# A second SwiGLU FFN on one core: where the differences and splits of the hidden tiles are queued

## The chip, the cores and the metric

The kernel runs on one core of one Trainium2 chip. A core has five engines, each with an instruction queue of its own that it works through in order: TensorE (PE in the profile; its weight loads are PEld), VectorE (DVE), ScalarE (ACT), GpSimd (POOL) and SyncE (SP). [...] The metric is the time of one execution on the device in microseconds; several executions are timed and the median is given. One more execution is recorded by the hardware profiler, and every view of the trace comes from that one.

## The reference, cut to what matters

One layer of a hybrid model in float32: 128 context tokens and 512 latent tokens (640 in all), 1024 channels; a SwiGLU FFN, a mixer, a second SwiGLU FFN, a last norm. The change is in the second FFN, whose hidden width is 2816.

```python
def swiglu(h, w1, w2):
    a, b = jnp.split(h @ w1, 2, axis=-1)
    return (jax.nn.silu(a) * b) @ w2

    h = modulate(rmsnorm(x, norm_g[2]), sh2, sc2)
    x = x + 0.5 * g2[:, None, :] * swiglu(h, ffn2_w1, ffn2_w2)
```

## The kernel before

**Products.** Channels lie on the 128 partitions, tokens on the free axis; the 640 tokens are two halves of 320. Each float32 operand is split into a high part (a cast to the type that TensorE reads, `A.copy` on ScalarE, line 75) and a low part (the difference, `V.tensor_sub` on VectorE, line 79). `three` (lines 245 to 247) multiplies high by high, high by low and low by high into the same accumulator `ps`.

**A pair.** Two weight columns (`mi` 0 and 1) times two token halves (`h` 0 and 1) is a 2 by 2 block product. `pair_steps` does it with seven products in place of eight, by sums and differences of blocks. The seven steps, numbered 0 to 6, are A11, S1, S2, A12, S3, S4, A22; each is 12 matmuls of 320 columns. The weight sums (`ws`, line 218) are made on VectorE, and each weight operand is split ahead of its use: the call of `op()` at a step queues the cast and the difference of the operand four steps on. The operands on the token side are tiles named 11, T1, T2, 21, T3, 22 and T4, in the order of the steps.

Between the products stand copies on ScalarE and additions on VectorE. After step 0 ScalarE copies the accumulator a to b (L273), which S2 then adds to; after step 1 it copies one to an SBUF tile (L279); after step 2 it copies b to c (L283), which S3 adds to. L294 (or L291 and L292) and L297 are additions on VectorE after S3 and S4. The results go through `ev`. Two of them are put off (the list `late`) and run by `flush()` behind the next pair's L273. Four accumulators rotate, so that a product may have to wait until an old one has been read; the one that S1 writes is free when L297 of the pair before has read it.

**Groups of eight.** In the second FFN the hidden width runs in groups of 8, 8 and 6 tiles. `eights` builds the first two: eight hidden tiles j, each a pair with the two halves of its w1 columns (tiles 0 and 1 of group 0 are done elsewhere, in the head, so `n_head` is 2), and then four pairs with w2 (m = 0, 2, 4, 6). The results of the hidden tiles are the token operands of the w2 pairs, so their differences are needed as well, and each operand is split. That work is put in the list `lazy` as closures: `left` and `diff1` for tiles 0 to 3 (one cast and one VectorE operation; one cast and two), `diff2`, `diff3` and `diff4` for tiles 4 to 7 (one cast and two VectorE operations each). They are added to `lazy` when a pair's results are complete, which is at `flush()` in step 0 of the next pair. T3 and T4 go to tiles lent from other operands (`put_lent`).

**When `lazy` runs.** In `pair_el`, a pair that is not `calm` calls `relax(7 - i)` behind step i from 1 on: it runs closures until fewer than 7 − i are left, so two closures run behind steps 5 and 6, three behind steps 4, 5 and 6. A dictionary `at` gives functions to be called behind a step, after that. In the last tile (j = 7), step 4 runs all of `lazy` (tile 6's closures) and three splits to lent tiles; step 6 runs `flush` and again all of `lazy` (tile 7's closures). Then the first w2 pair begins, whose step 0 does the fourth split to T3.

Of the kernel before, what the change touches and what calls it, by code (L numbers as in the profile page):

```python
# [44 lines left out]
def mixer_step(ctx: ExitStack, tc: tile.TileContext, x_prompt, x_sample, state_C, state_n, state_m,  # L45
# [23 lines left out]
    def t3():  # L69
        return tp.tile([P, HT], F32, name="t3", bufs=8)  # L70
# [3 lines left out]
    def split(raw, hi, lo, owe=False):  # L74
        A.copy(hi, raw)  # L75
        if owe:
            owed.append(lambda: V.tensor_sub(lo, raw, f32(hi)))
        else:
            V.tensor_sub(lo, raw, f32(hi))  # L79
# [8 lines left out]
    def drain(left=0):  # L88
        while len(fill) > left:
            fill.pop(0)["emit"]()  # L90
# [88 lines left out]
    def element(raws_, ops_, emit):  # L179
        return {"raws": raws_, "ops": ops_, "emit": emit}  # L180
# [19 lines left out]
    def w_load(w, row0, nk, col0, ncol):  # L200
        def load(t):
            nc.sync.dma_start(t[:, :nk * P].rearrange("p (k n) -> p k n", k=nk),
                              dap(w, row0 * ncol + col0, [[ncol, P], [P * ncol, nk], [1, P]]))
        return load
# [6 lines left out]
    def pair_ops(r1=0, r2=1, e1=None):  # L211
        e1 = e1 or V

        def total(key, engine, fn, a, b):
            def src(o):
                g = o["group"].setdefault(r1, {})
                t = g[key] = ring.tile([P, 512], F32, name="ws", bufs=SB)
                getattr(engine, fn)(t, part(o, a), part(o, b))  # L218
                return t
            return src  # L220

        def part(o, key):
            if key[0] == "S":
                return o["group"][r1][key]
            return rtile[o["base"] + (r1 if key[1] == "1" else r2)][:, LH if key[2] == "1" else RH]

        whole = lambda key: lambda o: part(o, key)
        spec = lambda src, *r: {"raws": list(r), "n": 512, "src": src}
        return {
            "A11": spec(whole("A11"), r1), "A12": spec(whole("A12"), r1), "A22": spec(whole("A22"), r2),  # L230
            "S1": spec(total("S1", e1, "tensor_add", "A21", "A22"), r2),
            "S2": spec(total("S2", V, "tensor_sub", "S1", "A11"), r1, r2),
            "S3": spec(total("S3", e1, "tensor_sub", "A11", "A21"), r1, r2),
            "S4": spec(total("S4", V, "tensor_sub", "A12", "S2"), r1, r2),
        }
# [13 lines left out]
    late, lazy, soon = [], [], []  # L249
# [5 lines left out]
    def relax(left=1):  # L255

        while lazy and len(lazy) >= left:
            lazy.pop(0)()

    def pair_steps(order, ev, spare_v, acts):  # L260
# [44 lines left out]
    def pair_el(load1, load2, ev, e1=None, spare_v=False, acts=HB, at=None, calm=False):  # L305
        po = pair_ops(e1=e1)
        at = at or {}

        def emit():
            nf = len(fill)  # L310
            for i, _ in enumerate(pair_steps(ORDER, ev, spare_v, acts)):
                if not calm:
                    relax(7 - i if i else 9)
                drain(nf - nf * (i + 1) // 7)
                for f in at.get(i, ()):
                    f()
        return dict(element([load1, load2], [po[name] for name in ORDER], emit), pair=True)
# [91 lines left out]
    def blocks_of(p):  # L409
        return [(p[i], lambda h, ps, i=i: p[2](i, h, ps)) for i in range(2)]  # L410
# [86 lines left out]
    at = 0  # L497
# [288 lines left out]
    def upair():  # L786
        return (PO["u"].tile([P, HT], F32R, name="Uh", bufs=PO["un"]),
                PO["u"].tile([P, HT], F32R, name="Ul", bufs=PO["un"]))
# [4 lines left out]
    def hpair(o):  # L793
        return (hpool(o).tile([P, HT], F32R, name="H" + o + "h", bufs=4),
                hpool(o).tile([P, HT], F32R, name="H" + o + "l", bufs=4))
# [162 lines left out]
    def x_back(m, x):  # L958
        G.dma_start(x, xd[m])

    def x_away(m, x):
        G.dma_start(xd[m], x)
# [7 lines left out]
    def h_back(o):  # L970
        for k in range(4):
            HB[o][k] = hpair(o)
            for i in range(2):
                G.dma_start(HB[o][k][i], hd[o, k, i])

    def eights(w1, w2, g, f0, n_head, head, more, back):

        spare = (n_head, n_head + 1, 7) if f0 < n_head else (7,)
        UB = {o: [None] * 4 for o in OPS_H}

        def tile_of(m):
            if "xs" not in PO:
                PO["xs"] = [xp.tile([P, T], (F32, F32R)[i // 4], name="x", bufs=KT) for i in range(KT)]
            return PO["xs"][m]
        slot = lambda a, k: tile_of(2 * a + k // 2)[:, hsl(k % 2)]
        raw3 = lambda k: slot(0, k)
        raw2 = lambda k: slot(1, k)

        def put_own(o, k, src):
            UB[o][k] = hl = upair()  # L990
            split(src, *hl)

        def put_22(k, src):
            UB["22"][k] = hl = [tile_of(4 + k)[:, hsl(i)] for i in range(2)]
            split(src, *hl)

        def put_lent(o, k, src):
            UB[o][k] = hl = hpair(o)
            split(src, *hl)

        def ev_of(j):
            sa, k = {}, j % 4

            def left():
                put_own("11", k, sa[0])

            def diff1():
                V.tensor_sub(raw2(k), raw3(k), sa[0])
                put_own("T1", k, raw2(k))

            def diff2():
                V.tensor_sub(raw2(k), sa[1], raw2(k))
                put_own("T2", k, raw2(k))

            def diff3():
                put_own("21", k, sa[0])
                V.tensor_sub(raw3(k), sa[1], raw3(k))

            def diff4():
                put_22(k, sa[1])  # L1020
                V.tensor_sub(raw2(k), sa[0], raw2(k))

            def ev(mi, h, src):
                if mi == 0:
                    sa[h] = raw3(k) if h and j < 4 else t3()
                    A.activation(sa[h], src, AF.Silu)
                    return
                V.tensor_mul(sa[h], src, sa[h])
                if h == 0:
                    if j < 4:  # L1030
                        lazy.append(left)
                else:
                    lazy.extend([diff1] if j < 4 else [diff2, diff3, diff4])
            return ev
        grp = []
        for j in range(8):
            p = (w_load(w1, 0, KT, (f0 + j) * P, 2 * DFF), w_load(w1, 0, KT, DFF + (f0 + j) * P, 2 * DFF), ev_of(j))
            at = {}
            if j == 7:
                lent = lambda k: lambda: put_lent("T3", k, raw3(k))  # L1040
                at = {4: [relax, lent(0), lent(1), lent(2)], 6: [flush, relax]}
            if f0 + j < n_head:
                head.extend(blocks_of(p))
            else:
                grp.append(pair_el(*p, at={**at, **more.get(j, {})}, spare_v=j in spare, calm=f0 + j == n_head))
        w2s = []
        away = lambda *ms: [lambda m=m: x_away(m, tile_of(m % 4)) for m in ms]
        come = lambda *ms: [lambda m=m: x_back(m, tile_of(m % 4)) for m in ms]
        PO["x_end"] = away(6, 7)
        for m in range(0, KT, 2):  # L1050
            ev = lambda mi, h, src, m=m: add_x(m + mi, h, src, g, False, tile_of((m + mi) % 4))
            at = {}
            if m == 0:
                four = lambda k: lambda: put_lent("T4", k, raw2(k))
                at = {0: [lambda: put_lent("T3", 3, raw3(3))], 1: come(0, 1) + [four(0)],
                      2: [four(1)], 3: [four(2), four(3)] + come(2, 3)}
            else:
                at = {1: away(m - 2, m - 1)}
                if m + 2 < KT:
                    at[2] = come(m + 2, m + 3)  # L1060
                else:
                    at[4] = [lambda: h_back("T3")] if back else []
                    at[6] = [lambda: h_back("T4")] if back else []
            w2s.append(pair_el(w_load(w2, f0 * P, 8, m * P, D), w_load(w2, f0 * P, 8, (m + 1) * P, D), ev,
                               spare_v=True, acts=UB, at=at))
        return grp, w2s
# [382 lines left out]
    def hsl(h):  # L1449
        return slice(*HALVES[h])  # L1450
# [669 lines left out]
    def x_whole():  # L2120
        for m in range(KT):
# [3 lines left out]
    more = {0: {3: {0: [lambda: h_away("T3", "T4")]}},  # L2125
            1: {0: {1: x_end}}, 2: {0: x_in_last}}
# [40 lines left out]
```

## Time and profile before

| | us |
|---|---|
| median of 3 runs | 1658.01 |
| lowest, highest | 1657.32, 1660.03 |
| the profiled execution | 1660.07 |
| its span, first to last instruction | 1658.2 |

Stretches of the second FFN in the trace, from the pair's first matmul:

| stretch | starts at us |
|---|---|
| group 0, tile 4 | 1265.51 |
| group 0, tile 5 | 1279.22 |
| group 0, tile 7 | 1303.83 |
| group 0, w2 pair 0 | 1316.14 |
| group 1, tile 1 | 1385.09 |
| group 1, tile 6 | 1446.62 |
| group 1, w2 pair 0 | 1471.23 |

How to read the views: a row of the order of time has the start in us, the duration of one, the engine, the line of the kernel, the operation, what it writes and reads, the shape, the count, and in brackets how long the engine stood idle before it and what ended that. Durations of neighbours overlap, so the distance of two starts is what an engine needs for one. `Uh`, `Ul` are tiles of high and low parts, `wh`, `wl` those of the weights; `x` and `t` hold results and differences.

### The profile page before, as it was taken

To read this page: it belongs to the slowest core of one execution; us is meant where nothing else is said; L and a number is where in the kernel's file an instruction comes from. 1 tells how busy PE (TensorE), PEld (TensorE's weight loads), DVE (VectorE), ACT (ScalarE), POOL (GpSimd) and SP (SyncE) were. 2 spreads that over 40 slices of the span, in tenths; PEclk is the share of its full clock that TensorE was granted. 3 is DMA by queue.
4 is the path that set the end of the run, shared out by engine and by line. 5 is a ranking of instruction groups with operands and counts; after the bars stand their busy time and mean duration, and the time that the engine had idled before them with its cause. 6 is when DMAs were issued, how large, how long until landed. Compare 5 with 4: busy or idle time off the path is not lost.

```text
span 1658.2 us, 29450 instructions
## 1 busy us (share of the span) xinstructions
PE 1631.9 (98%) x11093; PEld 1589.7 (96%) x11093; DVE 1320.3 (80%) x2786; ACT 825.0 (50%) x1805; POOL 221.9 (13%) x354
## 2 busy tenths in 40 slices
PE   8999999999999999999999999999999899999998
PEld 5999999999999999999999999999999899989998
DVE  6867877877778878788897898789598887898765
ACT  5642542543566556555561455533275544554543
POOL 2010000000031322121121211011121012003002
PEclk9999999999999999999999999999999999999999
DMA  9454343343353434342367423367355265237522
GB/s 321 114 164 123 106 123 111 102 129 100 107 184 84 113 89 101 76 118 67 96 200 237 117 77 90 106 189 215 90 172 140 79 197 164 77 116 213 176 80 64
DMA packets 283661, 216.68 MB, mean 131 GB/s; under 512 B 9331, under 2 KB 260602, under 8 KB 283520
## 3 DMA queue, kind: packets, MB, share of 16 engines
q1 hardware_dynamic: 263152, 158.36, 33.3%
q0 software_dynamic: 20336, 56.45, 11.5%
q8 instruction: 87, 1.43, 0.4%
q14 instruction: 54, 0.44, 0.1%
q10 hardware_dynamic: 32, 0.01, 0.0%
HBM read 188.98 MB, written 25.79 MB: 130 GB/s over the span
## 4 chain that ended last, share of the span: by engine, by line
PE 89%; DVE 5%; ACT 3%; DMA 2%; SPq 1%; issue 1%; POOL 0%; ACTq 0%; DVEq 0%; POOLq 0%
PE ps L245 27%; PE ps L246 27%; PE ps L247 27%; PE ax L1707 2%; PE ax L1738 2%; DVE wl L79 1%; DMA wr<-in_ffn_w_dram 1%; PE ax L1710 1%; ACT wh L75 1%; PE ax L1684 1%; ACT Uh L860 1%; DMA wh<-in_x_sample_dram 0%; DVE ws L218 0%; DVE Uh L852 0%; PE ax L709 0%
## 5 line engine op out<-in xcount | busy, mean ns | idle before, releaser
L79 DVE TENSOR_TENSOR wl<-wr,wh 128x512 fp32r<-128x512 f32 (+1 forms) x389 | 261.2, 683 | 79.2 <-ACT wh L75 76.0
L75 ACT CAST wh<-wr 128x512 fp32r<-128x512 f32 (+1 forms) x391 | 230.4, 600 | 89.2 <-PE ps L246 70.8
L79 DVE TENSOR_TENSOR wl<-ws,wh 128x512 fp32r<-128x512 f32 x324 | 228.3, 705 | 37.2 <-ACT wh L75 36.3
L75 ACT CAST wh<-ws 128x512 fp32r<-128x512 f32 x324 | 198.4, 619 | 104.6 <-DVE ws L218 64.7
L245 PE MATMUL ps<-Uh,wh 128*128 128x320 f32 x576 | 182.0, 316 | 8.3 <-ACT ps L273 6.2
L246 PE MATMUL ps<-Ul,wh 128*128 128x320 f32 x576 | 179.5, 312 | 0.0
L247 PE MATMUL ps<-Uh,wl 128*128 128x320 f32 x576 | 179.4, 312 | 0.0
L245 PE MATMUL ps<-HT4h,wh 128*128 128x320 f32 x408 | 128.4, 315 | 0.0
L246 PE MATMUL ps<-HT4l,wh 128*128 128x320 f32 x408 | 126.2, 309 | 0.1
L247 PE MATMUL ps<-HT4h,wl 128*128 128x320 f32 x408 | 126.1, 309 | 0.0
L245 PEld LDWEIGHTS ps<-Uh,wh 128*128 128x128 f32 x576 | 109.7, 191 | 10.5 <-ACT ps L273 6.8
L245 PE MATMUL ps<-H11h,wh 128*128 128x320 f32 x376 | 118.8, 316 | 0.5 <-ACT H11h L75 0.5
L245 PE MATMUL ps<-H21h,wh 128*128 128x320 f32 x376 | 117.7, 313 | 0.0
L246 PE MATMUL ps<-H11l,wh 128*128 128x320 f32 x376 | 116.5, 310 | 0.3
L247 PE MATMUL ps<-H21h,wl 128*128 128x320 f32 x376 | 116.2, 309 | 0.0
L247 PE MATMUL ps<-H11h,wl 128*128 128x320 f32 x376 | 116.2, 309 | 0.0
L246 PE MATMUL ps<-H21l,wh 128*128 128x320 f32 x376 | 116.0, 308 | 0.0
L245 PE MATMUL ps<-HT3h,wh 128*128 128x320 f32 x356 | 111.6, 313 | 0.0
L246 PE MATMUL ps<-HT3l,wh 128*128 128x320 f32 x356 | 110.0, 309 | 0.0
L247 PE MATMUL ps<-HT3h,wl 128*128 128x320 f32 x356 | 110.0, 309 | 0.0
L246 PEld LDWEIGHTS ps<-Ul,wh 128*128 128x128 f32 x576 | 109.8, 191 | 0.0
L247 PEld LDWEIGHTS ps<-Uh,wl 128*128 128x128 f32 x576 | 109.7, 190 | 0.0
(477 smaller groups left out, 4696.3 us busy)
## 6 DMA issues: line engine op xcount, KB each, us to landing
wr<-in_ffn_w_dram SPq DMA_DIRECT2D x102, 512.0 KB, 4.0
wr<-in_w_in_dram SPq DMA_DIRECT2D x72, 512.0 KB, 3.9
wr<-in_w_mod_dram SPq DMA_DIRECT2D x51, 512.0 KB, 3.8
wr<-in_ffn_w_dram SPq DMA_DIRECT2D x32, 384.0 KB, 3.4
xd<-x POOLq DMA_DIRECT2D x32, 320.0 KB, 5.5
x<-xd POOLq DMA_DIRECT2D x32, 320.0 KB, 4.2
early<-in_w_mod_dram SPq DMA_DIRECT2D x13, 512.0 KB, 8.8
mg<-in_w_mod_dram POOLq DMA_DIRECT2D x8, 512.0 KB, 5.5
```

Of the source, the lines that this page charges most:

```text
L75: A.copy(hi, raw)
L79: V.tensor_sub(lo, raw, f32(hi))
L245: PE.matmul(ps, hi[:, ws], ah, start=start, stop=False, skip_group_check=True)
L246: PE.matmul(ps, hi[:, ws], al, start=False, stop=False, skip_group_check=True)
L247: PE.matmul(ps, lo[:, ws], ah, start=False, stop=stop, skip_group_check=True)
L860: A.activation(t[:, a:b], t[:, a:b], AF.Identity, scale=sc_, bias=bi_)
L1684: PE.matmul(p[:, :P], S["k", dt][:, sl], S["q", dt][:, sl], start=(dt == 0), stop=(dt == 1))
L1707: PE.matmul(p2[:, :DH + 1], S["q", dt][:, sl], S["C"][d][:, dt, :], start=(dt == 0), stop=(dt == 1))
L1710: PE.matmul(p1[:, :DH + 1], S["p", ch][:, d, :], PO["vt"][:, ch, :], start=True, stop=True)
L1738: PE.matmul(p[:, :DH + 1], kw[:, dt * P:(dt + 1) * P], PO["vt"][:, ch, :], start=True, stop=True)
```

## The change

```diff
+    def joined(a, b):
+        return {i: [*a.get(i, ()), *b.get(i, ())] for i in {*a, *b}}
+
+    def relax_some(n):
+        for _ in range(min(n, len(lazy))):
             lazy.pop(0)()
...
             at = {}
             if j == 7:
                 lent = lambda k: lambda: put_lent("T3", k, raw3(k))
-                at = {4: [relax, lent(0), lent(1), lent(2)], 6: [flush, relax]}
+                at = {4: [lent(0), lent(1), lent(2)], 6: [flush]}
+            due = j - n_head if f0 < n_head else 8
+            if due:
+                at[1] = [relax if due > 2 else lambda n=due + 2: relax_some(n)]
...
-                grp.append(pair_el(*p, at={**at, **more.get(j, {})}, spare_v=j in spare, calm=f0 + j == n_head))
+                grp.append(pair_el(*p, at=joined(at, more.get(j, {})), spare_v=j in spare, calm=True))
...
             if m == 0:
                 four = lambda k: lambda: put_lent("T4", k, raw2(k))
-                at = {0: [lambda: put_lent("T3", 3, raw3(3))], 1: come(0, 1) + [four(0)],
+                at = {0: [relax], 1: [lambda: put_lent("T3", 3, raw3(3))] + come(0, 1) + [four(0)],
                       2: [four(1)], 3: [four(2), four(3)] + come(2, 3)}
```

All w1 pairs of the two groups are now calm: nothing of `lazy` runs behind their later steps. Instead it runs behind step 1, in one batch: all of it in every tile of group 1 and from tile 5 on in group 0; in group 0, tile 2 runs nothing (as before), tile 3 the first three closures and tile 4 the next four, out of a list that holds eight at tile 3, among them what the head left. The closures of a group's last tile no longer run behind its own step 6: `flush` still adds them to the list there, and they run behind step 0 of the first w2 pair, after that pair's L273. The fourth split to T3 moves from step 0 to step 1 of that pair. `joined` merges two dictionaries of such calls without losing either.

More of the change, by code (lines that the diff above doesn't have):

```diff
@@ L257, in relax @@
         while lazy and len(lazy) >= left:
+            lazy.pop(0)()
+    def joined(a, b):
+        return {i: [*a.get(i, ()), *b.get(i, ())] for i in {*a, *b}}
+    def relax_some(n):
+        for _ in range(min(n, len(lazy))):
             lazy.pop(0)()
```

## The prediction

> **What bounds the kernel now.** I read the page first, then the waits of TensorE alone, then TensorE's order of time in the stretch that the diff touches.
>
> ```profile
> PE 1631.9 (98%) x11093; PEld 1589.7 (96%) x11093; DVE 1320.3 (80%) x2786; ACT 825.0 (50%) x1805; POOL 221.9 (13%) x354
> ```
>
> TensorE is busy for 98% of the span, so a change of queue order on VectorE (DVE) and ScalarE (ACT) can only win what TensorE waits, or loses by a lower clock. The waits of TensorE from 1225 to 1600 us, the second FFN (us in total, times, longest):
>
> ```profile
> PE ps L245 <- ACT ps L273: 7.4, 3, 3.2
> PE ps L245 <- DVE t L297: 2.0, 2, 1.0
> ```
>
> Five waits in 375 us, on two lines. The order of time says where; the windows (us, then busy time of PE, PEld, DVE, ACT, POOL, then TensorE's granted clock) say what each stretch lost.
>
> ```profile
> 1270.32 0.41 PE L245 MATMUL ps<-HT2h,wh 128*128 128x320 f32 x1 [1.13 <-ACT ps L273]
> ...
> 1316.14 0.31 PE L245 MATMUL ps<-Uh,wh 128*128 128x320 f32 x1
> ...
> 1319.07 0.42 PE L245 MATMUL ps<-Uh,wh 128*128 128x320 f32 x1 [1.01 <-DVE t L297]
> ...
> 1324.26 0.63 PE L245 MATMUL ps<-Uh,wh 128*128 128x320 f32 x1 [3.15 <-ACT ps L273]
> ...
> 1330.55 0.31 PE L245 MATMUL ps<-HT3h,wh 128*128 128x320 f32 x1
> ```
>
> ```profile
> 1279.22:1291.53 12.31, 12.31 (x87) 12.31 (x85) 10.59 (x20) 6.20 (x14) 0.00 (x0) 1.00 0.31 87
> 1265.51:1279.22 13.71, 12.58 (x86) 12.33 (x85) 10.49 (x21) 7.61 (x17) 0.00 (x0) 1.00 0.27 78
> 1316.14:1330.55 14.41, 10.25 (x50) 9.72 (x49) 12.54 (x27) 8.72 (x20) 1.63 (x3) 0.76 0.33 90
> 1471.23:1484.44 13.21, 9.12 (x50) 8.59 (x49) 12.20 (x26) 8.28 (x20) 1.63 (x3) 0.87 0.30 78
> 1324.26:1330.05 5.79, 5.79 (x22) 5.79 (x23) 5.10 (x11) 4.35 (x11) 1.09 (x2) 0.50 0.56 147
> 1480.30:1483.70 3.40, 3.40 (x15) 3.40 (x15) 3.40 (x8) 3.27 (x8) 0.54 (x1) 0.51 0.66 169
> ```
>
> The first window is a pair without a wait: 12.31 us for seven products, 1.76 each. The second, tile 4 of group 0, takes 13.71: **1.40 lost**. The third and fourth run from the first product A11 of w2 pair 0 to its fifth, S3: four products, 7.03 us undisturbed. They take 14.41 and 13.21: **7.38 and 6.18 lost** at the two group ends. Idle time is only part of that: after the long wait the granted clock was 0.50 for 5.79 us and 0.51 for 3.40 us. All of it together is 14.96 us, the most that the change can win here.
>
> Both engines around the first group end:
>
> ```profile
> 1316.72 1.29 DVE L79 TENSOR_TENSOR HT3l<-x,HT3h 128x320 fp32r<-128x320 f32 x3
> ...
> 1318.53 0.48 DVE L297 TENSOR_TENSOR t<-ps,t 128x320 f32<-128x320 f32 x1
> ...
> 1321.66 0.49 DVE L1012 TENSOR_TENSOR x<-t,x 128x320 f32<-128x320 f32 x1
> 1322.19 0.46 ACT L75 CAST Uh<-x 128x320 fp32r<-128x320 f32 x1 [2.16 <-DVE x L1012]
> 1322.55 0.45 ACT L75 CAST Uh<-t 128x320 fp32r<-128x320 f32 x1
> 1322.68 0.49 DVE L79 TENSOR_TENSOR Ul<-x,Uh 128x320 fp32r<-128x320 f32 x1 [0.52 <-ACT Uh L75]
> 1322.91 0.45 ACT L75 CAST x<-t 128x320 fp32r<-128x320 f32 x1
> 1323.09 0.49 DVE L79 TENSOR_TENSOR Ul<-t,Uh 128x320 fp32r<-128x320 f32 x1
> 1323.27 0.61 ACT L75 CAST wh<-ws 128x512 fp32r<-128x512 f32 x1
> 1323.79 0.41 ACT L273 COPY ps<-ps 128x320 f32<-128x320 f32 x1
> ```
>
> ScalarE stood for 2.16 us at a cast that waits for diff2 of the last tile (L1012), with the copy L273 that S2 needs queued three casts behind it. diff2 itself was late since VectorE was still at the batch that the old step 4 puts down. So the waits are a matter of order, not of capacity, and order is what the diff changes.
>
> From the same rows come the prices that I use below. Next on ScalarE after a 320-column cast: 0.36 (1322.19 to 1322.55); after a 512-column one 0.52. On VectorE 0.41 after a 320-column operation. VectorE's result to ScalarE's start 0.52 (1321.66 to 1322.19), a cast to VectorE's difference 0.49, L273 to TensorE 0.47.
>
> **The change part by part.** No operation is added or removed: the same differences, casts and DMAs run. What moves is when they are queued. A pair in which nothing deferred is queued ahead shows the base, tile 1 of group 1:
>
> ```profile
> 1385.09 0.31 PE L245 MATMUL ps<-H11h,wh 128*128 128x320 f32 x1
> ...
> 1386.88 0.48 DVE L1028 TENSOR_TENSOR t<-ps,t 128x320 f32<-128x320 f32 x1
> ...
> 1388.08 0.69 DVE L79 TENSOR_TENSOR wl<-ws,wh 128x512 fp32r<-128x512 f32 x1 [0.32 <-ACT wh L75]
> ...
> 1388.80 0.43 ACT L279 COPY t<-ps 128x320 f32<-128x320 f32 x1 [0.76 <-PE ps L247]
> 1389.13 0.62 ACT L75 CAST wh<-wr 128x512 fp32r<-128x512 f32 x1
> ...
> 1390.56 0.41 ACT L283 COPY ps<-ps 128x320 f32<-128x320 f32 x1 [0.81 <-PE ps L247]
> ...
> 1392.12 0.31 PE L245 MATMUL ps<-HT3h,wh 128*128 128x320 f32 x1
> ```
>
> Counted from the pair's start: L1028 at +1.79, the last weight difference before the new place at +2.99 (VectorE free at +3.59), copy L279 at +3.71 (ScalarE free at +4.04), copy L283 at +5.47, S3 at +7.03. The new batch stands between L279 and the weight cast that precedes L283. L283 must start by 7.03 − 0.47 = +6.56, or S3 waits. That is the new risk in every inner pair, and I walk each size of batch through it.
>
> *Three closures (diff2 to 4; tiles 6, 7 of group 0 and 5 to 7 of group 1).* First difference +3.59, its cast +4.11, two more casts, free at +5.19, weight cast to +5.71, L283 +5.71: TensorE's slack is 0.85. Cost nil. The six VectorE operations are through at about +6.6, so L297 at the pair's end comes when S4 ends, and L1028 of the next pair at +1.79, which keeps the base valid.
>
> *Two closures (left, diff1; tiles 1 to 4 of group 1).* Cast of left +4.04; its difference +4.53, diff1 +4.94, cast +5.46 to +5.82, weight cast to +6.34, L283 +6.34: slack 0.22. Nil, but thin.
>
> *Tile 3 of group 0* gets the first three of eight closures, as before, and then nothing more; the other five go to the next tiles. *Tile 4* gets four (diff1, left, diff1, left), and no longer has L273 behind the old leftovers: its 1.40 us go. Two of the four casts wait for VectorE: casts at +4.11, +4.47, +5.86, +6.22; weight cast +6.58; L283 +7.10; S3 at +7.57: **0.54 lost**. *Tile 5* gets six (diff1, left, diff1, diff2, diff3, diff4), a chain that goes back and forth: casts +4.11, +4.47, +5.86, +7.26, +7.62, +7.98; weight cast +8.34; L283 +8.86; S3 at +9.33: **2.30 lost**. VectorE is then about 1.5 us behind and ends the addition L294 that A22 needs 0.4 late: **2.70 in all**. Before, this pair lost nothing. Bounds of the two: nothing, if casts pass faster than the row's 0.52 hand-over says, and 5, if VectorE enters them a weight split and a sum late. I take the walked 3.24.
>
> Does a 2.3 us gap also lower the clock? In the windows a gap of 3.15 us did, and at tile 4 one of 1.13 did not (PEclk 1.00). One slow stretch at half the clock for 3.40 us (row above) costs about 1.5. I take nothing, since the trace has no such gap.
> [...]
>
> *Group ends.* Step 4 of the last tile keeps three splits to lent tiles, without diff2 to 4 of tile 6 (six VectorE operations, 2.4 us) ahead of them. L297 is then at +11.75 of that pair, 0.5 before the w2 pair starts, and S1's wait of 1.01 goes. In the w2 pair, counted from its start: L1028 twice +1.56, a sum and a weight difference, VectorE free at +3.56; L273 goes out as soon as A11 ends, +1.96, ahead of all three closures, so S2 starts at +3.52 on time. The closures: diff2 at +3.56, cast +4.08, its difference done for TensorE at +5.04; S2 uses this tile's operand in its last quarter, the cast from +3.52 + 1.32 = +4.84, the difference from +4.99: 0.05 late. Behind them ScalarE has two casts, a weight cast, L279, the fourth T3 split (moved here from step 0), a T4 split, a weight cast, and only then L283, at about +7.24: S3 at +7.71 instead of 7.03: **0.7 lost per group end**. Nil if VectorE comes one split earlier; 2 if it comes 1.3 late. The moved split and closures also stand ahead of DMAs:
>
> ```profile
> wr<-in_ffn_w_dram SPq DMA_DIRECT2D x102, 512.0 KB, 4.0
> ...
> x<-xd POOLq DMA_DIRECT2D x32, 320.0 KB, 4.2
> ```
>
> On POOL's queue the second x tile of the w2 pair may be fetched only when the fourth T3 split has read its place, at about +7.6; it lands 4.2 later, and the next pair's flush reads it at about +13.9: hidden by 2 us, and a late one would hold VectorE, whose next customer on TensorE is 3 us further. On SP's queue a weight tile may be fetched when the last split of an old one is through; in tile 5 that split is 4.3 later than in the quiet pair (+8.34 against +4.04), and its ring of five tiles runs two pairs, over 20 us, ahead of a load that takes 4.0. Both cost nothing; without that cover, the 4.3 once.
>
> Sum: 14.96 − 3.24 − 1.4 = 10.3 us. The profiled execution took 1660.07, so 1649.8; the ratio 0.9938 on the median of 1658.01 gives **1647.7**.
>
> **The rivals.** *Clock falls in tile 5*: 1.5 to 2.6 more (the second window lost 2.6 over 5.79 us), 1649.3 to 1650.5. For it: both gaps of about 3.1 us that the trace has were followed by one. Against it: this gap is a quarter shorter, and the one of 1.13 was not followed by any. *The wait only changes place at the group ends*: ScalarE's row of eight before L283 is long; with 2 to 2.5 per end instead of 0.7, and a dip of the clock at one of them, 1651 to 1653. *Tiles 4 and 5 hide their batches*, because VectorE is earlier there: 1644.5. *Slower*: VectorE is already behind when the batch comes, in every pair. Before, it was, as tile 6 of group 1 shows:
>
> ```profile
> 1446.62 0.31 PE L245 MATMUL ps<-H11h,wh 128*128 128x320 f32 x1
> ...
> 1451.24 0.48 DVE L1028 TENSOR_TENSOR t<-ps,t 128x320 f32<-128x320 f32 x1
> ...
> 1452.05 0.68 DVE L79 TENSOR_TENSOR wl<-ws,wh 128x512 fp32r<-128x512 f32 x1
> ```
>
> L1028 at +4.62 instead of +1.79, VectorE free at +6.03. A batch queued there would cost 2.44 − 0.85 = 1.6 in each of five pairs of three, 1.2 in each of four pairs of two, 2.4 more in tiles 4 and 5: 17.7, and the kernel would take 1665. It decides from a lag of 1.8 us on. Against it: that lag came from the closures queued at the old steps 4 to 6, ahead of the next pair's sums, and these places are empty now; the quiet pair shows what is then left. *Nothing moves*: would need that S2 waits for the late operand as long as it waited for L273; the walk gives 0.05.
>
> **How the numbers follow.** Forecast, 1646 to 1649: 0.56. Clock falls: 0.15. Wait changes place: 0.11. Hidden: 0.08. Slower: 0.06. Nothing moves: 0.04. The range leaves out the last two and the outer ends: 1644 to 1653. A difference of under 0.2% (3.3 us) is about what a measurement of this kernel can't tell from no change; all but the last two cases lie beyond it: faster 0.90, same 0.04, slower 0.06.
>
> **What would show it.** Right: among TensorE's waits L297 is gone and L273 too, or under 0.3; the copy L283 takes their place, longest in tile 5 (about 2.3), then 0.5 to 0.7 in tile 4 and at both group ends; the two windows of A11 to S3 take about 7.7 each, at clock 1.00; L1028 stands at about +1.8 in all inner pairs. Wrong: waits on L283 in tiles 6 and 7 or in group 1's inner pairs, which would say that VectorE's lag stayed; a granted clock under 1.00 in tile 5; or S2's wait at a group end turned into one on L79 (the low part of T2).

## The result and the profile after

| | before | after |
|---|---|---|
| median of 5 runs, us | 1659.82 | 1652.16 |
| lowest, highest | 1657.32, 1660.79 | 1650.70, 1652.88 |
| the profiled execution | 1660.07 | 1651.78 |
| its span | 1658.2 | 1649.9 |
| its mean granted clock | 0.996 | 0.999 |

The ratio is 0.9957, with a 95% interval of 0.9942 to 0.9971: faster by 0.43%. The forecast was a ratio of 0.9938 and 1647.7 us; the time lies inside the range of 1644 to 1653, near its upper end, while the forecast ratio lies just outside the measured interval: the forecast gain was too large by almost half. Between the two profiled executions the gain is 8.29 us where the walk gave 10.3.

The busy time of each engine, from the page of the kernel after:

```profile
PE 1628.9 (99%) x11093; PEld 1585.9 (96%) x11093; DVE 1319.5 (80%) x2786; ACT 826.4 (50%) x1805; POOL 223.3 (14%) x354
```

The counts are those of before, and VectorE and ScalarE are as busy as they were. All of the gain is time in which TensorE waited (5.3 us less idle) or ran at a lower clock (3.0 us less busy). Its waits after, from 1225 to 1600 us (us in total, times, longest). The diff shifts the lines of the code by 7: L280 is the old L273, L290 the old L283, L301 the old L294, L304 the old L297, L1035 the old L1028.

```profile
PE ps L245 <- ACT ps L290: 3.5, 4, 2.2
PE ps L246 <- DMA HT4l<-hd: 0.4, 1, 0.4
PE ps L245 <- DVE t L301: 0.2, 1, 0.2
```

The waits on the copy after A11 (7.4 us before) and on the addition after S4 (2.0) are gone. In their place stand four waits on the copy that S3 adds to. TensorE's order of time says where they are (in brackets, idle time before the matmul and what ended it):

```profile
1273.42 0.42 PE L245 MATMUL ps<-HT3h,wh 128*128 128x320 f32 x1 [0.75 <-ACT ps L290]
1288.24 0.41 PE L245 MATMUL ps<-HT3h,wh 128*128 128x320 f32 x1 [2.22 <-ACT ps L290]
1292.22 0.41 PE L245 MATMUL ps<-HT4h,wh 128*128 128x320 f32 x1 [0.20 <-DVE t L301]
1326.63 0.41 PE L245 MATMUL ps<-HT3h,wh 128*128 128x320 f32 x1 [0.27 <-ACT ps L290]
1475.32 0.41 PE L245 MATMUL ps<-HT3h,wh 128*128 128x320 f32 x1 [0.28 <-ACT ps L290]
1530.28 0.42 PE L246 MATMUL ps<-HT4l,wh 128*128 128x320 f32 x1 [0.39 <-DMA HT4l<-hd]
```

Two in group 0 (tiles 4 and 5), one in the first w2 pair of each group. The windows (us, then busy time of PE, PEld, DVE, ACT, POOL, then the granted clock) give what each stretch takes: tile 4, tile 5 and tile 6 of group 0, and A11 to S3 at the two group ends.

```profile
1265.47:1278.81 13.34, 12.59 (x87) 12.32 (x86) 11.16 (x22) 7.50 (x17) 0.00 (x0) 1.00 0.28 81
1278.81:1294.08 15.27, 12.84 (x86) 12.32 (x85) 13.06 (x26) 8.11 (x18) 0.00 (x0) 1.00 0.24 70
1294.08:1306.39 12.31, 12.31 (x87) 12.31 (x85) 11.02 (x22) 7.28 (x17) 0.00 (x0) 1.00 0.28 85
1318.69:1326.63 7.94, 7.55 (x51) 6.99 (x49) 6.96 (x17) 5.56 (x14) 0.00 (x0) 1.00 0.37 107
1467.47:1475.32 7.85, 7.47 (x50) 6.97 (x49) 6.87 (x16) 5.55 (x14) 0.00 (x0) 1.00 0.37 109
```

Against the undisturbed 12.31 and 7.03:

| lost, us | before | walked for after | after |
|---|---|---|---|
| group 0, tile 4 | 1.40 | 0.54 | 1.03 |
| group 0, tile 5 | 0 | 2.70 | 2.96 |
| group 0 end | 7.38 | 0.7 | 0.91 |
| group 1 end | 6.18 | 0.7 | 0.82 |
| sum | 14.96 | 4.64 | 5.72 |

So 9.24 of the 14.96 us came back in these stretches. The bracket of a row is less than what a wait costs (0.75 against 1.03 in tile 4): it counts from the recorded end of the matmul ahead, 0.31 behind its start, while undisturbed matmuls start 0.15 apart. The distance of two starts is the better measure. At the group ends it also shows a second loss, which has no bracket and so stands in no list of waits. In S2, the low part of the last tile's diff2 comes late (VectorE's row, then TensorE's two around it):

```profile
1323.48 0.49 DVE L79 TENSOR_TENSOR Ul<-x,Uh 128x320 fp32r<-128x320 f32 x1 [0.53 <-ACT Uh L75]
...
1323.53 0.38 PE L245 MATMUL ps<-Uh,wh 128*128 128x320 f32 x1
1324.03 0.42 PE L246 MATMUL ps<-Ul,wh 128*128 128x320 f32 x1
```

The matmul that reads it starts 0.50 behind the one ahead, 0.06 after VectorE is done. With the slower start of the matmul behind it that is 0.47 of the 0.91 lost; S3's wait is the other 0.43. At the second group end it is 0.37 and 0.44.

### The profile page after: what moved, and what is told of

Read it like the earlier page. It is cut to its first block, busy times and chain, and to the rows that moved or that the text cites. A ratio compares the mean times of both kernels' runs of the same rounds, so it can differ in the third digit from the quotient of the medians.

```text
span 1649.9 us, 29478 instructions
## 1 busy us (share of the span) xinstructions
PE 1628.9 (99%) x11093; PEld 1585.9 (96%) x11093; DVE 1319.5 (80%) x2786; ACT 826.4 (50%) x1805; POOL 223.3 (14%) x354
## 4 chain that ended last, share of the span: by engine, by line
PE 89%; DVE 4%; ACT 3%; DMA 2%; issue 1%; POOL 0%; SPq 0%; ACTq 0%; DVEq 0%
PE ps L245 27%; PE ps L246 27%; PE ps L247 27%; PE ax L1717 2%; PE ax L1748 2%; PE ax L1720 1%; DVE wl L79 1%; ACT wh L75 1%; ACT Uh L867 1%; DMA early<-in_w_mod_dram 1%; DMA HT4l<-hd 1%; PE ax L1694 1%; DMA wr<-in_ffn_w_dram 0%; ACT Uh L75 0%; DVE Uh L859 0%
## 5 line engine op out<-in xcount | busy, mean ns | idle before, releaser
L79 DVE TENSOR_TENSOR wl<-wr,wh 128x512 fp32r<-128x512 f32 (+1 forms) x389 | 261.4, 684 | 79.8 <-ACT wh L75 77.5
L75 ACT CAST wh<-wr 128x512 fp32r<-128x512 f32 (+1 forms) x391 | 230.2, 600 | 89.1 <-PE ps L246 69.3
L79 DVE TENSOR_TENSOR wl<-ws,wh 128x512 fp32r<-128x512 f32 x324 | 228.0, 704 | 39.5 <-ACT wh L75 38.7
L75 ACT CAST wh<-ws 128x512 fp32r<-128x512 f32 x324 | 199.0, 620 | 108.9 <-DVE ws L218 71.4
```

## The experiments

Two theories stood against each other. **Order**: each wait is a copy on ScalarE queued behind a chain of casts and differences, its size follows from the number of closures in the batch and the step they are put behind, and the inner pairs are quiet because nothing queued late in one pair makes VectorE late in the next. **Ends only**: the gain is that at the group ends the copy L280 no longer stands behind the casts, and the inner batches are not needed for it. Behind these stood a question of size: how much can the losses of tiles 4 and 5 be lowered. All diffs are against the kernel after. Every experiment does the whole computation.

### Each half of the change alone

`e1_ends` keeps the new order at the group ends and puts the inner closures back behind the late steps:

```diff
-            due = j - n_head if f0 < n_head else 8
-            if due:
-                at[1] = [relax if due > 2 else lambda n=due + 2: relax_some(n)]
+            if j == 7:
+                at[1] = [relax]
...
-                grp.append(pair_el(*p, at=joined(at, more.get(j, {})), spare_v=j in spare, calm=True))
+                grp.append(pair_el(*p, at=joined(at, more.get(j, {})), spare_v=j in spare,
+                                   calm=f0 + j == n_head or j == 7))
```

> Only the group ends are changed: the last tile runs tile 6's closures behind step 1 and no others, the first w2 pair runs the last tile's closures behind L273. Tiles 3 to 6 of group 0 and 1 to 6 of group 1 are as before. My theory (what counts is the order of the queue, and a lag of VectorE that a pair enters is carried into it): the wait of 1.4 us in tile 4 stays, tile 5 loses nothing, the two group ends win about 6.4 and 5.4 as in the changed kernel; but tile 7 of each group is entered with the lag of the old steps 4 to 6 of tile 6 (L1028 about 4.6 us into the pair), so L283 is late there, 1.0 to 1.6 us in each group. Total against the kernel before: 8 to 10 us less. Rival (the batch at step 1 costs nothing whatever VectorE's state): no wait on L283 in tile 7, total about 11.7 us less. Rival (the group ends win only because the inner tiles are empty at steps 4 to 6): the waits L297 and L273 at the ends stay over half, total under 6 us less.

`e2_inner` is the other half, the new inner batches with the group ends as before:

```diff
-                at = {4: [lent(0), lent(1), lent(2)], 6: [flush]}
+                at = {4: [relax, lent(0), lent(1), lent(2)], 6: [flush, relax]}
...
-            if due:
+            if due and j < 7:
...
-                grp.append(pair_el(*p, at=joined(at, more.get(j, {})), spare_v=j in spare, calm=True))
+                grp.append(pair_el(*p, at=joined(at, more.get(j, {})), spare_v=j in spare, calm=j < 7))
...
-                at = {0: [relax], 1: [lambda: put_lent("T3", 3, raw3(3))] + come(0, 1) + [four(0)],
+                at = {0: [lambda: put_lent("T3", 3, raw3(3))], 1: come(0, 1) + [four(0)],
```

> Only the inner tiles are changed (3 to 6 of group 0, 0 to 6 of group 1, batch behind step 1); tile 7 and the first w2 pair as before. My theory: tile 4 wins 1.3 and loses 0.8, tile 5 loses 3.0, so tiles 3 to 6 of group 0 lose about 2.5 us in sum, nothing in group 1; at the group ends the wait on L273 stays over 2.5 us with its lower clock, the wait on L297 gets shorter or stays, since tile 7 begins without a lag. Total: 0 to 3 us more than before. Rival (the inner batches do most of the work of the change): total 4 us or more below before.

In a single run each, `e1_ends` took 1654.10 and `e2_inner` 1662.28, where the kernel before took 1659.32 in the median beside them (1657.86 to 1660.91). So `e1_ends` won 5.2 us and not the 8 to 10 expected; `e2_inner` is at the end of its 0 to 3 us more. TensorE's waits, first of `e1_ends`, then of `e2_inner`:

```profile
PE ps L245 <- ACT ps L290: 3.4, 4, 1.5
PE ps L245 <- ACT ps L280: 1.1, 1, 1.1
PE ps L245 <- ACT Uh L75: 1.0, 2, 0.5
```

```profile
PE ps L245 <- ACT ps L280: 6.3, 2, 3.2
PE ps L245 <- ACT ps L290: 3.0, 2, 2.2
PE ps L245 <- DVE t L304: 2.0, 2, 1.0
PE ps L245 <- DVE t L301: 0.2, 1, 0.2
```

`e2_inner` keeps both long waits at the ends (13.29 and 13.20 us from A11 to S3) and adds tile 5's: the inner batches alone win nothing. `e1_ends` brings the ends down to 8.66 and 8.59, 0.7 more than in the kernel after, since S2 waits there for the last tile's operand (the two waits on L75), and tile 4 keeps its 1.1. But a new loss came in tile 7 of both groups, 14.01 and 14.05 us in place of 12.31. There the lag shows that the rival on the slower side needed. Its rows in tile 7 of group 0: the pair's start, L1035, and S3.

```profile
1304.41 0.31 PE L245 MATMUL ps<-H11h,wh 128*128 128x320 f32 x1
...
1309.04 0.49 DVE L1035 TENSOR_TENSOR t<-ps,t 128x320 f32<-128x320 f32 x1
...
1313.04 0.41 PE L245 MATMUL ps<-HT3h,wh 128*128 128x320 f32 x1 [1.42 <-ACT ps L290]
```

The same pair in the kernel after:

```profile
1306.39 0.31 PE L245 MATMUL ps<-H11h,wh 128*128 128x320 f32 x1
...
1308.18 0.49 DVE L1035 TENSOR_TENSOR t<-ps,t 128x320 f32<-128x320 f32 x1
...
1312.12 0.41 ACT L290 COPY ps<-ps 128x320 f32<-128x320 f32 x1
```

L1035 at +4.63 with closures behind the late steps of the pair before, at +1.79 without. So neither half does it all: the ends are where the gain is, and the calm inner pairs are what lets a batch behind step 1 go through unnoticed. In the stretches named, `e1_ends` loses 8.0 us (tile 4, two tiles 7, two ends), the kernel after 5.7, the kernel before 15.0. "Ends only" fell with tile 7, "order" stood; the rival that expected under 6 us in all had the total, but not its waits on L280 and L304 at the ends, which are gone.

### What a batch costs

`e6_six` leaves out the batch of tile 5 in group 1, so that tile 6 there, quiet otherwise, gets six closures. If tile 5's loss in group 0 is the length of its chain and nothing special to that place, it appears here too:

```diff
-            if due:
+            if due and (f0 < n_head or j != 5):
```

> The changed kernel, but in group 1 tile 5 runs nothing of the deferred work and tile 6 runs six closures (diff2 to 4 of tiles 4 and 5) behind its step 1. No backlog of the head lies there, and VectorE is idle for a while in tile 5. My theory (the price is the length of the chain of one batch ahead of L283): a wait on L283 of 2.0 to 2.2 us at S3 of tile 6, no other wait in group 1's tiles beside up to 0.5 on the addition after S3 (L301); the granted clock stays at 1.00, since the gaps of 2.2 us seen so far did not lower it; total 2 to 2.8 us over the changed kernel. Rival (tile 5 of group 0 is slow because of the head's leftovers, not because of six closures): under 1 us. Rival (the clock falls after such a gap): a stretch of 3.4 us at 0.5, 1.5 us more.

```profile
1453.22 0.42 PE L245 MATMUL ps<-HT3h,wh 128*128 128x320 f32 x1 [2.02 <-ACT ps L290]
```

The pair took 15.06 us in place of 12.31, at a granted clock of 1.00: 2.75 lost, in a group where the kernel after loses nothing in that tile. The chain length makes the loss. In the whole it took 1655.06 in a single run, a little above the 2 to 2.8 us expected on top of the kernel after: in this execution the clock fell in tile 5 of group 0, which took 16.35.

`e7_later` puts the batches of tiles 3 to 5 of group 0 behind step 2, after the copy that S3 needs:

```diff
-                at[1] = [relax if due > 2 else lambda n=due + 2: relax_some(n)]
+                at[2 if due < 4 else 1] = [relax if due > 2 else lambda n=due + 2: relax_some(n)]
```

> The changed kernel, with the batches of tiles 3, 4 and 5 of group 0 behind step 2 (and so behind L283) instead of step 1. My theory: L283 is on time in all three, but VectorE does the closures ahead of the sums and weight differences of steps 3 and 4, so that the addition after S3 comes late and A22 waits for it (L301, in tiles 4 and 5, where VectorE reads the accumulator): little in tile 4, 2.5 to 4 us in tile 5; total 0 to 2 us over the changed kernel. Rival (only ScalarE's queue ahead of L283 counts): both waits go and nothing takes their place, 3.5 us less than the changed kernel.

```profile
1279.08 0.42 PE L245 MATMUL ps<-HT4h,wh 128*128 128x320 f32 x1 [1.17 <-DVE t L301]
1295.47 0.41 PE L245 MATMUL ps<-HT4h,wh 128*128 128x320 f32 x1 [3.82 <-DVE t L301]
```

The waits on L290 went and came back larger on L301, the addition on VectorE that the last product A22 needs: tiles 4 and 5 took 13.77 and 16.70. A single run took 1655.96, 3.8 us over the kernel after where 0 to 2 were expected. Of this, 1.23 us in tile 6 (13.54) are not the order but the clock, which fell behind the gap of 3.82: it was 0.52 from 1297.10 to 1300.50. Behind step 1 the batch holds ScalarE's queue (2.22 on L290 in tile 5), behind step 2 VectorE's (3.82 on L301); a chain of six is too long for either.

### A more even spread

`e3_spread` gives tiles 3 to 5 of group 0 shorter batches, the rest behind step 4 (each entry: tile, then step and number of closures):

```diff
+            parts = {3: {1: 3, 4: 2}, 4: {1: 2, 4: 1}, 5: {1: 2, 4: 3}}
...
-                at[1] = [relax if due > 2 else lambda n=due + 2: relax_some(n)]
+                few = parts.get(j) if f0 < n_head else None
+                at = joined(at, {i: [lambda n=n: relax_some(n)] for i, n in few.items()} if few else {1: [relax]})
```

> The changed kernel with the head's backlog dealt out in group 0: tile 3 three closures behind step 1 and two behind step 4, tile 4 two and one, tile 5 two and three; the rest as in the changed kernel. My theory (the length of one batch ahead of L283 is the price): the waits on L283 in tiles 4 and 5 (0.75 and 2.22 us) and the 0.20 on L294 go, tile 6 may lose up to 0.3 because VectorE enters it about 1.3 us late; 3 to 3.7 us less than the changed kernel, about 1648.5. Rival (VectorE has too much to do in these tiles, wherever it stands): the wait comes back in another place, under 1.5 us won.

`e8_even` is the same with the work brought forward, at steps 1, 2 and 4 of tiles 3 and 4, so that tile 5 has only three closures left:

```diff
+            parts = {3: {1: 3, 2: 2, 4: 1}, 4: {1: 2, 2: 1, 4: 1}}
```

> The head's backlog dealt out over tiles 3 and 4 of group 0, as VectorE's idle time there allows: tile 3 three closures behind step 1, two behind step 2, one behind step 4; tile 4 two, one, one; from tile 5 on three in one batch behind step 1, as in group 1. My theory: no wait over 0.3 us in tiles 3 to 6 of group 0, so 3.4 to 3.8 us less than the changed kernel, about 1648. Rival (group 0's tiles hold more VectorE work than fits, so that some 2 us are lost in whatever order): a wait of 1 us or more in tile 4, 5 or 6.

| kernel | median of 5, us | ratio to before, 95% | tile 4 | tile 5 | tile 6 | group ends |
|---|---|---|---|---|---|---|
| after | 1652.16 | 0.9957 [0.9942, 0.9971] | 13.34 | 15.27 | 12.31 | 7.94, 7.85 |
| `e3_spread` | 1650.07 | 0.9944 [0.9930, 0.9958] | 12.42 | 12.33 | 14.42 | 7.93, 7.85 |
| `e8_even` | 1648.44 | 0.9936 [0.9922, 0.9950] | 12.49 | 13.34 | 12.33 | 7.92, 7.86 |

`e3_spread` cleared tiles 4 and 5 and lost 2.11 in tile 6, where at most 0.3 was expected; it won 2.1 us and not 3 to 3.7. The pair's start, L1035 and S3 there:

```profile
1291.58 0.31 PE L245 MATMUL ps<-H11h,wh 128*128 128x320 f32 x1
...
1296.15 0.48 DVE L1035 TENSOR_TENSOR t<-ps,t 128x320 f32<-128x320 f32 x1
...
1300.15 0.42 PE L245 MATMUL ps<-HT3h,wh 128*128 128x320 f32 x1 [1.16 <-ACT ps L290]
```

L1035 at +4.57: three closures behind step 4 make VectorE late by 2.8 us in the next pair, the same lag as in `e1_ends`. In `e8_even` only one stands there, in tiles 3 and 4. The next pair lags too, as tile 5's start and L1035 show:

```profile
1277.99 0.31 PE L245 MATMUL ps<-H11h,wh 128*128 128x320 f32 x1
...
1281.49 0.48 DVE L1035 TENSOR_TENSOR t<-ps,t 128x320 f32<-128x320 f32 x1
```

L1035 is at +3.50, and a batch of three, free elsewhere, costs 1.03 here, against the 2.96 of six in the kernel after. It is the closure behind step 4 that lags, and not those behind step 2: `e3_spread` has one behind step 4 of tile 4 and none behind step 2, and L1035 of tile 5 stands at +3.17; in `e7_later` three and four behind step 2 of tiles 3 and 4 left it at +1.80 and +1.95 in the next pair. The total came as expected (3.4 to 3.8 us less). This kernel is the fastest measured: its runs (1648.02 to 1648.51) lie below all of the kernel after's.

### The group ends

`e4_splits` moves two splits of the first w2 pair from step 1 to step 2, behind the copy L290:

```diff
-                at = {0: [relax], 1: [lambda: put_lent("T3", 3, raw3(3))] + come(0, 1) + [four(0)],
-                      2: [four(1)], 3: [four(2), four(3)] + come(2, 3)}
+                at = {0: [relax], 1: come(0),
+                      2: [lambda: put_lent("T3", 3, raw3(3))] + come(1) + [four(0), four(1)],
+                      3: [four(2), four(3)] + come(2, 3)}
```

> The changed kernel with the fourth T3 split and the first T4 split of the first w2 pair moved from behind step 1 to behind step 2, so that they stand behind L283 (the fetch of the second x tile moves with them). My theory (the two casts ahead of L283 make it late): L283 starts about 0.7 us earlier after the pair's start, the wait of 0.27 at S3 of both group ends goes and the window A11 to S3 falls from about 7.9 to 7.1 or 7.3; 1.2 to 1.8 us less in all. Rival (S3 waits because VectorE's chain is late, not ScalarE's row): the window stays at 7.7 or more, or S3's last quarter waits for T3 instead.

A11 to S3 went from 7.94 and 7.85 to 7.46 and 7.42, short of the 7.1 to 7.3 expected. S3's wait is gone, as it should be if those splits made L290 late; what stays is S2's wait on the low part of diff2. The same stretch of the next w2 pair went from 7.11 to 7.57 and 7.59, with two new waits on L280. The loss only changes its place: about 0.5 less here, about 0.5 more behind it, and 1651.48 in a single run where 1.2 to 1.8 us less were expected. What holds L280 in the next pair is a cast that waits for a weight sum on VectorE:

```profile
1334.80 0.62 ACT L75 CAST wh<-ws 128x512 fp32r<-128x512 f32 x1 [2.08 <-DVE ws L218]
...
1335.33 0.42 ACT L280 COPY ps<-ps 128x320 f32<-128x320 f32 x1
```

This L280 stands at +16.30 from the start of the first w2 pair, and at +16.32 in the kernel after, so with either order; from 1323.79 on VectorE has no idle time up to it (in the kernel after from 1323.48). So VectorE sets the pace here, and moving these splits can't mend it.

Then VectorE's work itself should go down. `e10_pool` and `e11_sums` are `e8_even` with two of the four weight sums (L218) of that pair on GpSimd; `e10_pool` has the order of `e4_splits` as well:

```diff
-                               spare_v=True, acts=UB, at=at))
+                               e1=None if m else G, spare_v=True, acts=UB, at=at))
```

> The kernel with the evenly dealt backlog (e8), the two splits behind L283 as in e4, and two of the four weight sums of the first w2 pair of each group made on GpSimd (1.34 us each there, in other stages) instead of VectorE, where they take 0.60 each just ahead of the group end. My theory (what is left at the group ends, 0.9 us each, is VectorE's load: 1.2 us less of it and the wait neither stays at S3 nor moves to the next pair): the window A11 to S3 falls to 7.1, the next pair waits under 0.1, 1.4 to 1.8 us less than e8, about 1646.8. Rival (GpSimd's sums slow VectorE while they run, or come late themselves, since its queue also holds the x tiles' fetches): no gain, or a wait on a cast of ws.

> As e10, but with the two splits left where the changed kernel has them, ahead of L283. My theory: VectorE is 1.2 us earlier with diff2, so ScalarE's row of casts ahead of L283 begins 1.2 us earlier and L283 is on time: window A11 to S3 7.1 to 7.3, 1.2 to 1.7 us less than e8. Rival (ScalarE's row is too long whenever it starts): the wait of 0.27 and the 0.9 lost stay at S3.

They took 1651.11 (1650.45 to 1651.52) and 1650.59 (1650.28 to 1650.89), both slower than `e8_even`, where 1.2 to 1.8 us less were expected; the kernel before took 1659.04 in the median beside them (1658.79 beside `e8_even`). A11 to S3 took 7.61 and 7.54 in `e10_pool`, with 7.57 and 7.58 in the pair behind, and 8.04 and 7.97 in `e11_sums`, in place of the 7.1 to 7.3 expected. The order of time of VectorE and GpSimd in `e11_sums` says why:

```profile
1301.42 1.29 POOL L218 TENSOR_TENSOR ws<-wr 128x512 f32<-128x512 f32 x1 [48.81 <-DVE wl L79]
1301.64 1.62 DVE L79 TENSOR_TENSOR wl<-ws,wh 128x512 fp32r<-128x512 f32 x1
...
1306.69 1.29 POOL L218 TENSOR_TENSOR ws<-wr 128x512 f32<-128x512 f32 x1 [3.98 <-DVE wl L79]
1306.92 1.41 DVE L1035 TENSOR_TENSOR t<-t,t 128x320 f32<-128x320 f32 x1
```

Each of the two GpSimd sums of 1.29 us stretches the VectorE operation that runs beside it, from 0.69 to 1.62 and from 0.48 to 1.41 us, 0.93 each (0.69 and 0.48 are the same two in `e8_even`). A sum on VectorE takes 0.60 between two starts. The help costs VectorE more than it saves, and tile 7, in which the second of them runs, took 12.89 and 13.02 in place of 12.33 and 12.31. So on balance no run here took work off VectorE, and what that would do for the group ends stays open.
In both cases the VectorE operation starts 0.22 and 0.23 after GpSimd's and ends 0.55 and 0.35 after it. How the one holds up the other is not shown.

### The clock

The kernel after was profiled once more, to see which of its waits come back, and whether its 2.2 us gap in tile 5 is always free.

> The changed kernel once more. The wait of 0.39 us for the fetch of a T4 tile, near 1530 us, was in its first trace and in none of the other kernels' that run the same code there. If it belongs to the change, it is here again; if it is a matter of the memory traffic of one execution, it is gone or different. The waits on L283 in tiles 4 and 5 and at both group ends are here again within 0.1 us, at clock 1.00.

It gave 1652.18 (1651.12 to 1652.62), ratio 0.9958 [0.9946, 0.9971], and the same waits on L290, but neither the one on a DMA nor the 0.20 on L301. In tile 5, first the execution shown above, then this one (the window from S3 to A22):

```profile
1288.24:1292.22 3.98, 3.78 (x24) 3.52 (x24) 3.98 (x9) 2.07 (x4) 0.00 (x0) 1.00 0.42 117
```

```profile
1288.61 0.41 PE L245 MATMUL ps<-HT3h,wh 128*128 128x320 f32 x1 [2.23 <-ACT ps L290]
...
1288.61:1293.77 5.16, 5.16 (x25) 5.16 (x26) 4.53 (x9) 2.08 (x4) 0.00 (x0) 0.67 0.37 105
```

The same gap was followed by a clock of 1.00 in one execution and of 0.67 over 5.16 us in the other, and the pair took 16.36 in place of 15.27. Five profiled executions have this gap: it was followed by full clock in three (after, `e2_inner`, `e4_splits`: 2.22 to 2.24 us; in the last two the matmuls behind it start 0.15 apart) and by a fall in two (`e9_again`, `e6_six`: 2.23 and 2.24, 0.67 over 5.16 us in each). So at this length the gap alone doesn't decide it. Its neighbours: the four gaps of 3.08 to 3.17 us at the group ends and the one of 3.82 in `e7_later` were all followed by a fall (before: 0.50 over 5.79 us and 0.51 over 3.40; `e2_inner`: 13.29 and 13.20 us from A11 to S3, about 2 each over 7.03 and the idle times; `e7_later`: 0.52 over 3.40), the one of 2.02 in tile 6 of `e6_six` was not (1.00 over 3.98).

## Why the prediction held, and where it was off

**What bounds the kernel: right.** Order and not capacity: with the same operations and the same busy time, the waits on the copy after A11 and on the addition after S4 went, as forecast. Only what is left at the group ends is VectorE's load (`e4_splits`).

**Batches of two and three: right.** But for tile 3 of group 0, all such pairs take 12.30 or 12.31 us, even those with the thin slack of 0.22, and L1035 stands at +1.79 as walked (+1.95 in tile 6, behind the batch of six), L290 in tile 7 at +5.73 (1312.12 − 1306.39) where the walk had +5.71. Tile 3 takes 12.74, but took 12.77 before: other small matmuls (L597) stand in it. There L1035 is at +3.11 (+3.12 before), so the sign "+1.8 in all inner pairs" was not met in that one.

**Tile 5: right in its mechanism, 0.26 short.** ScalarE in that pair, which starts at 1278.81:

```profile
1282.92 0.46 ACT L75 CAST Uh<-x 128x320 fp32r<-128x320 f32 x1
...
1284.75 0.46 ACT L75 CAST Uh<-x 128x320 fp32r<-128x320 f32 x1 [1.00 <-DVE x L1015]
...
1286.17 0.46 ACT L75 CAST Uh<-x 128x320 fp32r<-128x320 f32 x1 [0.96 <-DVE x L1019]
...
1286.89 0.45 ACT L75 CAST x<-t 128x320 fp32r<-128x320 f32 x1
1287.25 0.61 ACT L75 CAST wh<-wr 128x512 fp32r<-128x512 f32 x1
1287.77 0.41 ACT L290 COPY ps<-ps 128x320 f32<-128x320 f32 x1
```

Casts at +4.11, +5.94, +7.36 and +8.08, the weight cast +8.44, L290 +8.96, S3 +9.43. The walk had +4.11, +5.86, +7.26, +7.98, +8.34, +8.86 and +9.33. Six hand-overs between two engines, worked out from two prices, came out 0.1 us late at the end; the rest of the 0.26 lies behind S3 (3.98 from S3 to A22, with the wait on L301, and 1.86 from there, in place of 3.52 and 1.76).

**Tile 4: the term "0.54 lost" was mis-sized, it measured 1.03.** The base was taken from a quiet pair in which L273 (now L280) starts at +2.01. In tile 4 VectorE enters the batch 0.3 later:

```profile
1267.27 0.48 DVE L1035 TENSOR_TENSOR t<-ps,t 128x320 f32<-128x320 f32 x1
1267.78 0.41 ACT L280 COPY ps<-ps 128x320 f32<-128x320 f32 x1 [1.84 <-PE ps L247]
...
1269.37 0.48 DVE L1015 TENSOR_TENSOR x<-x,t 128x320 f32<-128x320 f32 x1
```

Here L280 starts at +2.31, the weight casts and differences behind it move with it, and the first closure is at +3.90 instead of +3.59. S3 comes at +7.95, 0.38 behind the walk, and the rest of the loss lies behind S3. L280 starts 0.51 after L1035, which is the hand-over from VectorE to ScalarE of the prediction's rows; but that it waits for it there is not shown. In `e8_even` and `e3_spread` L280 starts at +2.01 and +2.02 in tile 4 with L1035 only behind it, at +3.22 and +3.39. What delays it by 0.3 stays open.

**Group ends: the term "0.7 lost per group end" was right to 0.2.** 0.91 and 0.82. diff2 of the last tile starts at +3.78, where the walk had it at +3.56:

```profile
1322.47 0.48 DVE L1019 TENSOR_TENSOR x<-t,x 128x320 f32<-128x320 f32 x1
```

That the sum fits so well is in part luck. The walk gave S2's late operand 0.05 and S3 the rest; it was 0.47 and 0.37 for S2, half of the loss or nearly so, and S3 lost less than walked. A wait of S2 on the low part of T2 (L79) was one of the prediction's own signs of being wrong, and here, in small, it came. What `e4_splits` added is that S3's part isn't one of place.

**The clock: "I take nothing" was half right, and the reason was wrong.** The forecast put the fall at a chance of 0.15, and argued by the length of the gap. It fell in two of five executions with one and the same gap, for 1.09 us in tile 5. Over both sets of timed runs of this kernel, three have a mean granted clock of 0.999 and took 1650.70 to 1651.78, three have 0.998 and took 1651.61 to 1652.88, and four have 0.997 and took 1652.16 to 1652.62; 0.997 and 0.999 occur in both sets. A forecast by expectation would have had about 0.4 us for it (two fifths of 1.09).

**The rest of the sum.** 10.3 were walked, 8.29 measured between the two profiled executions. Of the 2.0 us, tile 4 has 0.49, tile 5 0.26, the ends 0.33. The wait on HT4's transfer, which is in this trace alone and not in that of the second set, takes 0.66 with what follows it: it belongs to the execution, not to the change. The pairs behind the group ends are 0.16 later each, 0.33 together, a term the walk did not have: the first w2 pair passes a little of its load on (7.11 in the next one where 7.04 was before). The forecast time misses by more than this walk, 4.5 us. Another 1.8 come from its base, a median of 3 runs at 1658.01 where 5 gave 1659.82, and the last 0.6 from where the profiled executions lie among their runs. So that 1652.16 fell into the range was not the walk's doing alone: it lies in the stretch of 1651 to 1653 that was added for the rival *wait changes place*, and that rival's waits did not come.

**The rivals.** *Clock falls in tile 5* is true in some executions, at 1.09 us and not the 1.5 to 2.6 given (which on top of 1647.7 are 1649.2 to 1650.3, not quite the times stated). *The wait only changes place at the ends* fell, with 0.9 and 0.8 in place of 2 to 2.5; *tiles 4 and 5 hide their batches* fell, with 3.99 lost. *Slower, by a lag in every pair* did not come, and `e1_ends` shows why: with closures behind the late steps the lag is there (+4.63), and each batch that then stands behind step 1 cost 1.70 and 1.75, where the rival had 1.6 for a batch of three. *Nothing moves* fell with the group ends, 7.94 and 7.85 in place of 14.41 and 13.21.

## What to carry to other kernels

Where engines work through their queues in order, a wait is priced by walking the queue from a known start: count what stands ahead of the copy that the next product needs, and take each hand-over between two engines at its row (here 0.5 us). Put deferred work where its chain is over before that copy is due, in batches no longer than the slack (three closures here, where no lag is brought in), and not late in a stage: what is put there returns as a lag in the next one (L1035 at +4.57 and +4.63 here, in place of +1.79). When a wait moves to the next stage as soon as it is cleared (`e4_splits`), look for the engine that runs without a gap there; whether less work on it would help is not shown here.

## What the runs showed of the hardware that was not expected

**The clock after a gap of 2.2 us differs from execution to execution.** A gap of 2.2 us, identical to 0.02 us, was followed by a granted clock of 1.00 in three executions and of 0.67, over 5.16 us, in two. The two falls are from one set of runs, but the mean clocks of the timed runs differ within each set in the same way.
What decides it is not shown: the traces have the gap and the clock behind it.

**GpSimd's sums slowed VectorE.** In `e11_sums` a sum of 512 columns on GpSimd took 1.29 us, against 0.60 between two starts on VectorE, and the two VectorE operations beside such sums were 0.93 us longer each.
